# A hybrid encoder layer: normalised mixer operand, float32 SSM output operator, gates ahead of the attention, the per-layer projection moved to the FFN boundary

## The chip, the cores and the metric

The kernel runs on one core of one Trainium2 chip. The metric is device microseconds of one execution, the median of several runs. The engines are named PE (TensorE), DVE (VectorE), ACT (ScalarE), POOL (GpSimd) and SP (SyncE, which here only issues DMAs).

## The reference, cut to what is computed

One layer on 512 tokens of width 1024, all in float32:

```python
h = x
h = h + 0.5 * swiglu(rms_norm(h, ffn1_norm), ffn1_w_gate, ffn1_w_up, ffn1_w_down)   # width 2816
u = rms_norm(h, mix_norm)
q, k, v, x_ssm, g_attn, g_ssm = split(u @ w_in)          # 512, 128, 128, 512, 1024, 1024
q = rope(rms_norm(q)); k = rope(rms_norm(k))             # 8 query heads, 2 key/value heads of 64
y_attn = attention(q, k, v) @ w_attn_branch
y_s5 = s5_scan(x_ssm, forward) + s5_scan(x_ssm, reverse) + ssm_d * x_ssm   # 32 groups x 16, 64 states
z = gelu(y_s5)
z = z * sigmoid(z @ ssm_glu_w + ssm_glu_b)
y_ssm = z @ w_ssm_branch
h = h + (sigmoid(g_attn) * y_attn + sigmoid(g_ssm) * y_ssm) @ w_out
h = h + 0.5 * swiglu(rms_norm(h, ffn2_norm), ffn2_w_gate, ffn2_w_up, ffn2_w_down)
h = h + sigmoid(rms_norm(h, ple_norm) @ ple_w_gate) * (p @ ple_w_proj)     # p is 512 x 256
```

## The kernel before

**Layout and arithmetic.** The activation h is held transposed, features on partitions, as 8 tiles of 128x512. A large product works on float32r pairs: an operand is split into a high part, cast by ACT (L546), and a low part, subtracted by DVE (L547), and three matmuls (high by high, high by low, low by high; mm3, L560 to L563) go into one PSUM bank. wchunk (L549) loads a weight piece of at most 128x1024 over SP's queue (4 raw buffers, 4 split ones) and splits it so. The SSM's small products use bfloat16 triples with six matmuls (mm6, L43).

**Order.** Every engine has its own queue, in order. A scheduler fills the queues from the program's order as a priority; `tc.high_priority()` raises a piece, and a bank or a buffer with few copies holds its next user back. So the order that an engine sees differs from that of the code.

**Stages.** The input is loaded and transposed. FFN1 runs until 407.8 us; in its gaps a generator, ssm_params (L249 and after), computes the SSM's operators and writes them to DRAM: d_wv (input operator), d_wo (output operator), d_m (the part within a chunk) and d_tb (rotation and decay tables). Then the mixer:

- X, the SSM's input, is projected (proj_T, L785, 24 matmuls a tile, four tiles), goes to DRAM (xs_d) and comes back regrouped as U (L872), which is split into three bfloat16 parts (L875). rb, the row of 1/rms of all tokens, is made by the matmul pb from a diagonal matrix dg (L594 to L602) and multiplied in where a bank is copied out: X (L866), the gates (L816); K, V and Q take it per token as the scale of an ACT copy (L881, L883, L891).
- K and V, then Q, are projected with tokens on partitions (proj_tok, L801). Q and K get their head norm (msq, rqk, L894 to L897) and rope; both are transposed to qT, kh and kl. Q's head norm rq is not multiplied into Q but into the row maxima (L941) and the scale of the exponential (L943).
- Sixteen SSM blocks of two groups (ssm_block, L445): 24 bfloat16 matmuls pv, two rotations and two scans on DVE, a split of the state E into three bfloat16 parts (L481), then 12 matmuls with ml and 24 with wol into py; GELU writes a part of Z. ssm_prefetch (L428) loads a block's four operators over SP; wv has one buffer, the others two.
- The 16 gates (L812) are tanh of projections of 24 matmuls each. Eight (NG1) follow Q in the code, four (NG2) stand between the blocks, four fill the attention.
- The attention works head by head: scores (sc, L935 to L945), then values (L976): 16 transposes ppt, a split of each bank, eight matmuls po. Every head runs beside a filler, fill(i) (L1045): first the last four gates, then two halves of the GLU, whose operand zT comes from DRAM (z_load, L1007), then four halves of the SSM branch. The reciprocal row sums go to r_d (L949) and come back broadcast as R (L999), over SP; so do Z's stores (L966) and zT.
- The attention branch (96 matmuls) and w_out (192) end at 762.85 us.

FFN2 follows, and the tail: p is transposed (L1111), the gate product pge (192 matmuls) and the projection ple (48, L1143) are made per half of the width, combined (L1145 to L1148) and stored.

Of the kernel before, what the change touches and what calls it, by code (L numbers as in the profile page):

```python
# [45 lines left out]
def ssm_params(tc, nc, pk_, px, dp, k):  # L46
# [6 lines left out]
    d["wo"] = dp.tile([NB, P, 3 * GB * 2 * P], BF16, name="d_wo")  # L53
# [263 lines left out]
    bds = [pw.tile([P, 2, GB, 2, CH], F32, name=f"bd{i}") for i in range(2)]  # L317
# [110 lines left out]
def ssm_prefetch(nc, sp, k, j):  # L428
# [3 lines left out]
    wv = sp.tile([P, 3, GM, 2 * P], BF16, tag="wv", name=f"wv{j}")  # L432
# [768 lines left out]
```

## Time and profile before

| | |
|---|---|
| median of 3 runs | 1190.06 us (1187.46 to 1190.89) |
| the profiled execution | 1190.98 us, its span 1189.2 us |
| PE busy | 1145.6 us, 96% |
| DVE busy | 772.0 us, 65% |
| ACT busy | 501.6 us, 42% |
| POOL busy | 44.0 us, 4% |
| X's first and K's first matmul | 407.82, 431.43 us |
| first SSM product | 457.7 us |
| head 0's last score, attention's end | 583.49, 697.6 us |
| w_out's end | 762.85 us |

Times in the timeline count from the start of the span. A matmul's printed duration is longer than the distance to the next one, since matmuls overlap; where a dense stretch is priced, starts are subtracted. "Busy" of a group is the sum of its instructions, and the words behind the bar tell how long the engine had idled ahead of them and what ended that.

### The profile page before, as it was taken

How to read it: one execution, taken by the hardware profiler on the slowest of the kernel's cores; microseconds unless marked ns; L12 is line 12 of the kernel's file. 1: busy time of each engine (PE TensorE's matmuls, PEld its weight loads, DVE VectorE, ACT ScalarE, POOL GpSimd, SP SyncE). 2: the span in 40 equal slices, each digit the busy share in tenths (PEclk: the TensorE clock that was granted, in tenths of full speed). 3: DMA queues.
4: the chain of work that ended last, by engine and by line, in shares of the span. 5: the costliest groups of instructions: out<-in, count | busy, mean ns of one | idle time of the engine just before them, and what ended most of it. 6: DMA issues, size and time to landing. Idle time of an engine off the chain costs nothing.

```text
span 1189.2 us, 16474 instructions
## 1 busy us (share of the span) xinstructions
PE 1145.6 (96%) x6150; PEld 943.5 (79%) x6150; DVE 772.0 (65%) x1574; ACT 501.6 (42%) x915; POOL 44.0 (4%) x70
## 2 busy tenths in 40 slices
PE   8999989999999998988997999999999999999998
PEld 7788768888788887776785788888888888888886
DVE  4797589977688756999667857554443344444542
ACT  6475355544345435534465634333222223223331
POOL 4004300000000000000000000000000000000100
PEclk9999989999999999999998999999999999999999
DMA  9639956546967977887632135333323433223422
GB/s 199 142 93 275 283 181 199 173 137 138 280 216 259 280 195 145 243 257 228 162 95 51 45 85 172 89 100 96 90 63 97 140 91 105 79 72 98 154 59 53
DMA packets 258496, 175.97 MB, mean 148 GB/s; under 512 B 38928, under 2 KB 239824, under 8 KB 258416
## 3 DMA queue, kind: packets, MB, share of 16 engines
q1 hardware_dynamic: 254032, 162.66, 48.1%
q0 software_dynamic: 3920, 11.15, 3.7%
q10 hardware_dynamic: 464, 1.11, 0.4%
q8 instruction: 48, 0.79, 0.3%
q14 instruction: 32, 0.26, 0.1%
HBM read 148.89 MB, written 37.58 MB: 157 GB/s over the span
## 4 chain that ended last, share of the span: by engine, by line
PE 73%; DMA 10%; DVE 7%; SPq 3%; ACT 3%; issue 3%; ACTq 0%; DVEq 0%
PE pd L562 7%; PE pd L561 7%; PE pd L563 7%; PE pg L561 7%; PE pg L562 7%; PE pg L563 7%; PE pu L561 5%; PE pu L563 5%; PE pu L562 5%; DMA d_tb<-tst 3%; DMA wv<-d_wv 2%; DMA w<-in_ffn_w_up_dram 2%; PE pi L561 2%; PE pi L563 2%; PE pi L562 2%
## 5 line engine op out<-in xcount | busy, mean ns | idle before, releaser
L708 DVE TENSOR_TENSOR t<-pu,rb 128x512 f32<-128x512 f32 x44 | 30.3, 688 | 82.5 <-PE pu L563 82.3
L706 DVE TENSOR_TENSOR t<-pg,rb 128x512 f32<-128x512 f32 x44 | 30.3, 688 | 54.5 <-PE pg L563 52.5
L546 ACT CAST ah<-t 128x512 fp32r<-128x512 f32 x44 | 27.4, 622 | 42.3 <-DVE t L709 42.2
L726 DVE SCALAR_TENSOR_TENSOR h<-pd,h 128x512 f32<-128x512 f32 x32 | 22.0, 686 | 29.3 <-PE pd L563 29.3
L707 ACT ACTIVATE t<-t 128x512 f32<-128x512 f32 x44 | 27.8, 632 | 30.9 <-DVE t L706 30.3
L547 DVE TENSOR_TENSOR al<-t,ah 128x512 fp32r<-128x512 f32 x44 | 30.1, 685 | 7.1 <-ACT ah L546 7.0
L940 DVE TENSOR_REDUCE nb<-sc 128x1 f32<-128x512 f32 x32 | 21.6, 684 | 16.6 <-PE sc L939 16.5
L709 DVE TENSOR_TENSOR t<-t,t 128x512 f32<-128x512 f32 x44 | 30.3, 688 | 2.3
L943 ACT ACTIVATE p<-sc,nb,rq 128x512 f32<-128x512 f32 x32 | 24.8, 782 | 9.7 <-DVE nb L941 9.6
L547 DVE TENSOR_TENSOR pl<-ppt,ph 128x512 fp32r<-128x512 f32 x32 | 21.9, 684 | 6.6 <-ACT ph L546 6.6
L571 ACT ACTIVATE xh<-h,gains 128x512 fp32r<-128x512 f32 x24 | 17.4, 724 | 18.2 <-DVE h L726 17.8
L43 PE MATMUL pv<-U,wv 128*128 128x64 bf16 x384 | 14.0, 194 | 11.4 <-DMA wv<-d_wv 8.2
L1106 POOL DMA_DIRECT2D pin<-in_p_dram x8 | 4.2, 527 | 550.7 <-PE pd L562 545.5
L546 ACT CAST ph<-ppt 128x512 fp32r<-128x512 f32 x32 | 18.7, 589 | 12.8 <-PE ppt L983 12.6
L43 PEld LDWEIGHTS <-wv 128*128 128x128 bf16 x384 | 12.3, 98 | 14.3 <-DMA wv<-d_wv 10.0
L983 PE MATMUL ppt<-ident,p 128*128 128x128 f32 x128 | 20.6, 277 | 2.0 <-ACT p L943 2.0
L983 PEld LDWEIGHTS ppt<-ident,p 128*128 128x128 f32 x128 | 16.5, 142 | 6.7 <-ACT p L943 2.4
L33 ACT CAST E<-vv 128x256 bf16<-128x256 f32 x16 | 6.5, 403 | 32.1 <-DVE vv L479 31.9
L989 PE MATMUL po<-pl,vhl 128*128 128x512 f32 x32 | 13.5, 422 | 4.8 <-DVE pl L547 4.8
L43 PE MATMUL py<-E,wol 128*128 128x64 bf16 x384 | 17.7, 193 | 0.5 <-DVE E L36 0.4
L572 DVE SCALAR_TENSOR_TENSOR xl<-h,gains,xh 128x512 fp32r<-128x512 f32 x24 | 17.9, 746 | 0.4
L988 PE MATMUL po<-ph,vhl 128*128 128x512 f32 x32 | 14.2, 443 | 3.3 <-ACT ph L546 3.3
(1969 smaller groups left out, 3888.0 us busy)
## 6 DMA issues: line engine op xcount, KB each, us to landing
w<-in_ffn_w_gate_dram SPq DMA_DIRECT2D x44, 512.0 KB
w<-in_ffn_w_up_dram SPq DMA_DIRECT2D x44, 512.0 KB
w<-in_w_in_dram SPq DMA_DIRECT2D x26, 512.0 KB
w<-in_ffn_w_down_dram SPq DMA_DIRECT2D x32, 384.0 KB
w<-in_ffn_w_down_dram SPq DMA_DIRECT2D x32, 320.0 KB
d_wo<-wo SPq DMA_DIRECT2D x8, 768.0 KB
d_wv<-wv SPq DMA_DIRECT2D x8, 768.0 KB
wv<-d_wv SPq DMA_DIRECT2D x16, 384.0 KB
```

The lines of the kernel that those rows point to most:

```text
L43: nc.tensor.matmul(o, a[i], b[j], start=start and n == 0, stop=stop and n == 5)
L546: S.copy(hi, src)
L547: V.tensor_sub(lo, src, hi.bitcast(F32))
L561: T.matmul(o, ah, bh, start=start, stop=False)
L562: T.matmul(o, ah, bl, start=False, stop=False)
L563: T.matmul(o, al, bh, start=False, stop=stop)
L706: V.tensor_mul(t1, gu[0], rb)
L707: S.activation(t1, t1, AF.Silu)
L708: V.tensor_mul(t2, gu[1], rb)
L709: V.tensor_mul(t1, t1, t2)
L943: S.activation(p_, sc, AF.Exp, bias=nb[:, t:t + 1], scale=rq[:, t, hd:hd + 1], accum_out=sm[:, t:t + 1])
L983: T.transpose(pt[:, t * P:(t + 1) * P], pr[t][:, kt * P:(kt + 1) * P], ident)
```

## The change

- **Normalised operand.** FFN1's end no longer writes the split operand of h times the gain. It only collects squares; then rb is made, and behind it, in a new pool "pf", each tile xn = h x gain x rb is made and split. So X, K, V and Q are copied from their banks unscaled by ACT, and a gate is one tanh from the bank.
- **The projection of p** moves from the tail to this boundary: 8 transposes, 48 matmuls; eight results po of 128x512 (four buffers) are copied by ACT and stored to DRAM (pe_d) over POOL's queue. They are read back over the same queue ahead of FFN2, and the tail combines from there.
- **d_wo in float32.** One operator of 256 KB a block instead of three bfloat16 ones of 384 KB; E is not split; four float32 matmuls of 128x64 a block instead of 24 bfloat16 ones. The generator's store moves, wt gets two buffers and bd one.
- **wv** has two buffers.
- **NG2 is 8:** no gate is left among the heads, and block 0 is issued after Q's last matmul.
- **rq is multiplied into Q** (four DVE operations of 128x512); the 32 small multiplications of L941 and the scale of the exponential go.
- **POOL's queue** takes Z's stores, in quarters after blocks 3, 7, 11 and 15 (32 DMAs), zT's loads, r_d's stores and R's loads. z_load is cut in two, the loads one filler earlier than the splits; hb is loaded earlier.

The diff, cut to its core:

```diff
-    d["wo"] = dp.tile([NB, P, 3 * GB * 2 * P], BF16, name="d_wo")
+    d["wo"] = dp.tile([NB, P, GB * 2 * P], F32, name="d_wo")
...
-    wv = sp.tile([P, 3, GM, 2 * P], BF16, tag="wv", name=f"wv{j}")
+    wv = sp.tile([P, 3, GM, 2 * P], BF16, tag="wv", bufs=2, name=f"wv{j}")
...
-    wo = sp.tile([P, 3, GM, 2 * P], BF16, tag="wo", bufs=2, name=f"wol{j}")
+    wo = sp.tile([P, GM, 2 * P], F32, tag="wo", bufs=2, name=f"wol{j}")
...
-    E3 = [sp.tile([P, 2, N], BF16, tag=f"E{i}", bufs=2, name=f"E3{j}_{i}") for i in range(3)]
-    split3(nc, sp, E, E3, "vv", f"Er{j}", 3)
...
-            mm6(nc, o, [wo[:, i, g, ri * P:(ri + 1) * P] for i in range(3)],
-                [e[:, ri, g * NC_:(g + 1) * NC_] for e in E3], False, ri == 1)
+            nc.tensor.matmul(o, wo[:, g, ri * P:(ri + 1) * P], E[:, ri, g * NC_:(g + 1) * NC_],
+                             start=False, stop=ri == 1)
...
-NG1, NG2 = 8, 4
+NG1, NG2 = 8, 8
...
+        with tc.tile_pool(name="pf", bufs=1, reuse_waits="tile") as pp:
+            with tc.high_priority():
+                rb = rstd_bcast(st.rt())
...
+                    S.copy(po, pe)
+                    nc.gpsimd.dma_start(pe_d[t, :, nh * 512:(nh + 1) * 512], po)
+            xg = xg_tiles("x", KT)
+            with tc.high_priority():
+                for m in range(KT):
+                    xn = pp.tile([P, SEQ], F32, tag="xn", bufs=2, name=uid("xn"))
+                    V.scalar_tensor_tensor(xn, h[m], gains[:, 1, m:m + 1], rb, mul, mul)
+                    split(xg[m][0], xg[m][1], xn)
...
-            V.tensor_mul(dst, pg, rb)
-            S.activation(dst, dst, AF.Tanh, scale=0.5)
+            S.activation(dst, pg, AF.Tanh, scale=0.5)
...
+        for t in range(TT):
+            V.tensor_mul(qs[t], qs[t], rq[:, t].unsqueeze(2).broadcast_to([P, NH, HD]))
...
-            V.tensor_mul(nb[:, t:t + 1], nb[:, t:t + 1], rq[:, t, hd:hd + 1])
-            S.activation(p_, sc, AF.Exp, bias=nb[:, t:t + 1], scale=rq[:, t, hd:hd + 1], accum_out=sm[:, t:t + 1])
+            S.activation(p_, sc, AF.Exp, bias=nb[:, t:t + 1], accum_out=sm[:, t:t + 1])
...
-            nc.sync.dma_start(r_d[hd // 2].rearrange("h (t p) -> p h t", p=P), s2)
+            nc.gpsimd.dma_start(r_d[hd // 2].rearrange("h (t p) -> p h t", p=P), s2)
...
-        with tc.high_priority():
+        with tc.high_priority(), (tc.issue_after(last_q.ins) if j == 0 else ExitStack()):
...
+        if j % 4 == 3:
+            gs = slice((j - 3) * GM, (j + 1) * GM)
+            for l in range(L):
+                nc.gpsimd.dma_start(zv[l][:, gs], Z[l * CH:(l + 1) * CH, gs])
...
-                nc.sync.dma_start(R[i * HD:(i + 1) * HD], r_d[hd // 2][i].partition_broadcast(HD))
+                nc.gpsimd.dma_start(R[i * HD:(i + 1) * HD], r_d[hd // 2][i].partition_broadcast(HD))
...
-            nc.sync.dma_start(zT, zs_d[m * P:(m + 1) * P])
+            nc.gpsimd.dma_start(zTs[m], zs_d[m * P:(m + 1) * P])
...
+    pes = [lp.tile([P, D], F32, name=f"pes{t}") for t in range(TT)]
+    for t in range(TT):
+        nc.gpsimd.dma_start(pes[t], pe_d[t])
...
-                pe = bank("pv", uid("ple"))
-                for k in range(2):
-                    mm3(pe, pT[k][0][:, tk], pT[k][1][:, tk], ph[:, k], pl[:, k], k == 0, k == 1)
-                V.scalar_tensor_tensor(sg, sg, 1.0, pe, add, mul)
+                V.scalar_tensor_tensor(sg, sg, 1.0, pes[t][:, cs], add, mul)
```

What stands in the queues, first ACT's at the boundary between FFN1 and the mixer, before (w_... are weights' high parts, rb the row of 1/rms, ks and vs the copies of K and V):

```order
L546 CAST w_311h_4346<-w_311_4345 128x1024
L546 CAST w_312h_4400<-w_312_4399 128x1024
L546 CAST w_329h_4518<-w_329_4517 128x1024
L601 COPY rb_286_4114<-pb_285_4112 128x512
L546 CAST w_330h_4548<-w_330_4547 128x1024
L881 ACTIVATE ks0_4453<-pk0_4341,rs_282_4092 128x128
```

and after (po: the copies of the projection's banks ple; xh: high parts of the normalised operand):

```order
L794 COPY po_279_4130<-ple_278_4123 128x512
L794 COPY po_281_4140<-ple_280_4133 128x512
L794 COPY po_283_4150<-ple_282_4143 128x512
L794 COPY po_285_4160<-ple_284_4153 128x512
L544 CAST w_337h_4389<-w_337_4388 128x1024
L794 COPY po_288_4176<-ple_287_4169 128x512
L794 COPY po_290_4186<-ple_289_4179 128x512
L599 COPY rb_270_4085<-pb_269_4083 128x512
L794 COPY po_292_4196<-ple_291_4189 128x512
L544 CAST xh_295_4209<-xn_311_4225 128x512
```

rb stood behind weights' casts alone; now it stands behind six po copies, of which the fifth and sixth reuse the buffers of the first two.

SP's queue in the middle of the SSM blocks, before (tblN, wvN, mlN, wolN are block N's operators, w_... a gate's weights):

```order
L436 DMA tbl5_5599<-d_tb_282 128x5x128
L437 DMA tbl5_5599<-d_tb_282 128x128
L433 DMA wv5_5597<-d_wv_279 128x3x512
L441 DMA ml4_5509<-d_m_281 128x3x256
L556 DMA w_379_5384<-in_w_in_dram 128x8x128
L439 DMA wol4_5507<-d_wo_280 128x3x512
L436 DMA tbl6_5727<-d_tb_282 128x5x128
L437 DMA tbl6_5727<-d_tb_282 128x128
L433 DMA wv6_5725<-d_wv_279 128x3x512
```

and after, from block 2's wv on:

```order
L433 DMA wv2_5362<-d_wv_280 128x3x512
L433 DMA wv3_5429<-d_wv_280 128x3x512
L554 DMA w_393_5095<-in_w_in_dram 128x8x128
L436 DMA tbl2_5364<-d_tb_283 128x5x128
L437 DMA tbl2_5364<-d_tb_283 128x128
L433 DMA wv4_5528<-d_wv_280 128x3x512
L433 DMA wv5_5603<-d_wv_280 128x3x512
L441 DMA ml2_5369<-d_m_282 128x3x256
L439 DMA wol2_5367<-d_wo_281 128x512
```

Block N's wv stood behind block N's tables; now the wv of two blocks are asked for ahead of the tables of the first of them.

PE's queue where head 0's scores end and its transposes begin, before (sc: scores, ppt: transposes of the exponentials p, pi: a gate's bank):

```order
L938 MATMUL sc_393_6646<-kh_295_4139,qT_287_4131 128x512
L939 MATMUL sc_393_6646<-kl_297_4141,qT_287_4131 128x512
L983 MATMUL ppt_396_6752<-ident_69,p_388_6630 128x128
L561 MATMUL pi_400_6767<-xh_35_379,w_399h_6762 128x512
L562 MATMUL pi_400_6767<-xl_36_380,w_399h_6762 128x512
L563 MATMUL pi_400_6767<-xh_35_379,w_399l_6763 128x512
L561 MATMUL pi_400_6767<-xh_37_381,w_399h_6762 128x512
L562 MATMUL pi_400_6767<-xl_38_382,w_399h_6762 128x512
```

and after:

```order
L972 MATMUL sc_431_6505<-kh_327_4283,qT_319_4275 128x512
L973 MATMUL sc_431_6505<-kl_329_4285,qT_319_4275 128x512
L972 MATMUL sc_433_6511<-kh_327_4283,qT_319_4275 128x512
L973 MATMUL sc_433_6511<-kl_329_4285,qT_319_4275 128x512
L1018 MATMUL ppt_440_6596<-ident_69,p_428_6497 128x128
L972 MATMUL sc_444_6606<-kh_327_4283,qT_320_4276 128x512
L973 MATMUL sc_444_6606<-kl_329_4285,qT_320_4276 128x512
L1018 MATMUL ppt_446_6614<-ident_69,p_428_6497 128x128
L1018 MATMUL ppt_440_6596<-ident_69,p_430_6503 128x128
L1018 MATMUL ppt_446_6614<-ident_69,p_430_6503 128x128
```

The gate's matmuls that stood between head 0's transposes now stand ahead of its scores; behind them scores of head 1 alternate with the transposes.

## Rows read from the trace of the kernel before

**Rows 1.** The page's first part: busy time, share of the span, instructions.
```profile
PE 1145.6 (96%) x6150; PEld 943.5 (79%) x6150; DVE 772.0 (65%) x1574; ACT 501.6 (42%) x915; POOL 44.0 (4%) x70
```

**Rows 2.** Timeline, TensorE, 407 to 515: start us, us, engine line op operands.
```profile
407.59 0.39 PE L563 MATMUL pd<-ah,w_278l 128*128 128x512 f32 x1
...
415.75 0.95 PE L622 MATMUL pm<-ones,ss 128*128 128x1 f32 x8
...
416.56 0.49 PE L563 MATMUL pi<-xh,w_302l 128*128 128x512 f32 x1
...
428.94 1.02 PE L599 MATMUL pb<-dg,ones 128*128 128x512 f32 x2
...
442.97 0.40 PE L561 MATMUL pq<-w_329h,xh 128*128 128x512 f32 x1
...
513.79 0.86 PE L43 MATMUL pv<-U,wv 128*128 128x64 bf16 x24
...
514.49 0.34 PE L43 MATMUL py<-U,ml 128*128 128x64 bf16 x6
```

**Rows 3.** Timeline, VectorE and ScalarE, in the stretch of X.
```profile
423.08 0.16 DVE L584 TENSOR_TENSOR rs<-rs,rs 128x4 f32<-128x4 f32 x1
...
423.28 0.88 DVE L597 TENSOR_SCALAR dg<-ident,rs 128x128 f32<-128x128 f32 x4
...
430.00 0.59 ACT L601 COPY rb<-pb 128x512 f32<-128x512 f32 x1 [3.84 <-PE pb L599]
```

**Rows 4.** Timeline, TensorE, in the tail: first and last of 24 matmuls.
```profile
1178.27 0.39 PE L561 MATMUL ple<-w_1019h,pT 128*128 128x512 f32 x1
...
1183.48 0.39 PE L563 MATMUL ple<-w_1019h,pT 128*128 128x512 f32 x1
```

**Rows 5.** Stages: stretch, length, busy PE PEld DVE ACT POOL, granted clock, DMA share, GB/s.
```profile
431.43:583.72 152.29, 138.63 (x1473) 116.82 (x1472) 127.47 (x301) 68.58 (x195) 0.76 (x1) 0.98 0.77 206
583.72:697.60 113.88, 103.19 (x494) 82.35 (x494) 77.61 (x147) 68.56 (x133) 0.00 (x0) 0.96 0.32 71
484.00:514.00 30.00, 27.44 (x286) 22.48 (x285) 29.46 (x86) 11.88 (x36) 0.00 (x0) 1.00 0.85 255
514.00:544.00 30.00, 25.57 (x373) 21.85 (x369) 27.53 (x62) 13.32 (x28) 0.00 (x0) 1.00 0.90 262
623.00:643.00 20.00, 12.03 (x46) 8.59 (x45) 12.37 (x24) 10.10 (x21) 0.00 (x0) 0.74 0.38 56
```

**Rows 6.** Groups, 425 to 600: busy us, mean ns | idle before, releasers.
```profile
L477 DVE TENSOR_TENSOR te<-W,tbl 128x512 f32<-128x512 f32 x16 | 11.0, 685 | 0.1
...
L478 DVE TENSOR_TENSOR vv<-te 128x128 f32<-128x128 f32 x16 | 4.7, 291 | 0.2
...
L36 DVE TENSOR_TENSOR E<-Er,E 128x256 bf16<-128x256 f32 x16 | 6.8, 422 | 1.2 <-ACT E L35 0.9
...
L547 DVE TENSOR_TENSOR w_379l<-w,w_379h 128x1024 fp32r<-128x1024 f32 x1 | 1.2, 1225 | 0.5 <-ACT w_379h L546 0.5
...
L43 PE MATMUL py<-E,wol 128*128 128x64 bf16 x384 | 17.7, 193 | 0.5 <-DVE E L36 0.4
...
L43 PE MATMUL pv<-U,wv 128*128 128x64 bf16 x384 | 14.0, 194 | 11.4 <-DMA wv<-d_wv 8.2 <-DVE U L36 3.2
```

**Rows 7.** DMA issues of GpSimd's queue: count, KB each, median us to landing.
```profile
d_a<-d_at POOLq DMA_DIRECT2D x16, 256.0 KB, 10.8
...
d_bt<-sb POOLq DMA_DIRECT2D x2, 256.0 KB, 4.4
...
pin<-in_p_dram POOLq DMA_DIRECT2D x8, 64.0 KB, 2.4
```

**Rows 8.** Attention: a row of TensorE's timeline, two of the chain of waits.
```profile
585.88 0.33 PE L983 MATMUL ppt<-ident,p 128*128 128x128 f32 x1 [2.00 <-ACT p L943]
...
611.51 0.44 PE ppt L983 x4
...
622.27 11.60 DMA zT<-zs_d
```

More of the change, by code (lines that the diff above doesn't have):

```diff
@@ L316, in ssm_params @@
     kt = sm([P, 2, G, CH], "kt", pool=pk_)
-    bds = [pw.tile([P, 2, GB, 2, CH], F32, name=f"bd{i}") for i in range(2)]
+    bds = [pw.tile([P, 2, GB, 2, CH], F32, name=f"bd{i}") for i in range(1)]
     for bd in bds:
@@ L562, in mm3 @@
         T.matmul(o, ah, bl, start=False, stop=False)
-        T.matmul(o, al, bh, start=False, stop=stop)
+        return T.matmul(o, al, bh, start=False, stop=stop)
     def xg_tiles(tagp, n):
@@ L627 @@
     h_d = dp.tile([KT, P, SEQ], F32, name="h_d")
+    pe_d = dp.tile([TT, P, D], F32, name="pe_d")
     xg = xg_tiles("x", KT)
@@ L769 @@
             pass
-        xg = xg2
-        rt = st.rt()
-        rb = rstd_bcast(rt)
+        px_.close()
+        with tc.tile_pool(name="pf", bufs=1, reuse_waits="tile") as pp:
+            with tc.high_priority():
+                rb = rstd_bcast(st.rt())
+            pvw = w["p"][0, 0].rearrange("(c l) d -> l c d", l=L)
+            pin = [pp.tile([P, PLE], F32, name=f"pin{j}") for j in range(TT)]
+            for j in range(TT):
+                for i in range(2):
+                    nc.gpsimd.dma_start(pin[j][i * 64:(i + 1) * 64], pvw[2 * j + i])
+            pT = [tuple(pp.tile([P, SEQ], F32R, name=uid("pT")) for c in "hl") for k in range(2)]
+            for k in range(2):
+                pt = bank("pt", uid("pTp"))
+                for j in range(TT):
+                    T.transpose(pt[:, j * P:(j + 1) * P], pin[j][:, k * P:(k + 1) * P], ident)
+                split(pT[k][0], pT[k][1], pt)
+            for nh in range(2):
+                ph, pl = wchunk(w["ple_w_proj"][0][:, nh * 512:(nh + 1) * 512], 2, 512)
+                for t in range(TT):
+                    tk = slice(t * P, (t + 1) * P)
+                    pe = bank("mm", uid("ple"))
+                    for k in range(2):
+                        mm3(pe, pT[k][0][:, tk], pT[k][1][:, tk], ph[:, k], pl[:, k], k == 0, k == 1)
+                    po = pp.tile([P, 512], F32, tag="po", bufs=4, name=uid("po"))
+                    S.copy(po, pe)
[6 more added lines that the diff above has]
+                    split(xg[m][0], xg[m][1], xn)
     win = w["w_in"][0]
@@ L826 @@
     vhl = mp.tile([P, TT, 2, 2, HD], F32R, name="vhl")
-    rq = mp.tile([P, TT, NH], F32, name="rq")
     sx = ExitStack()
@@ L963 @@
             run(scores(0))
-    zv = zs_d.rearrange("(g c) (l n) -> l c g n", c=CH, l=L)
-    for l in range(L):
-        nc.sync.dma_start(zv[l], Z[l * CH:(l + 1) * CH])
     sx.close()
@@ L1048, in fill @@
             return gate(NG1 + NG2 + i)
-        if i < ng + 2:
-            if i == ng:
-                z_load()
-            return half(w["ssm_glu_w"][0], i - ng, [z[1:] for z in zs[1:]], glu_done)
-        if i < ng + 6:
-            return half(w["w_ssm_branch"][0], i - ng - 2, yhl, ssm_done)
+        i -= ng + 2
+        if i < 0:
+            if i == -2:
+                zl.append(z_load())
+            next(zl[0], None)
+            return iter(())
+        if i < 2:
+            return half(w["ssm_glu_w"][0], i, [z[1:] for z in zs[1:]], glu_done)
+        if i < 6:
+            return half(w["w_ssm_branch"][0], i - 2, yhl, ssm_done)
         return iter(())
@@ L1074 @@
         run(values(hd), fill(hd), *([scores(hd + 1)] if hd < NH - 1 else []))
-    for i in range(NH, 2 * KT - NG1 - NG2 + 6):
+    for i in range(NH, 2 * KT - NG1 - NG2 + 8):
         run(fill(i))
@@ L1090 @@
     mx.close()
+    lp = ctx.enter_context(tc.tile_pool(name="lp", bufs=1, reuse_waits="tile"))
+    pes = [lp.tile([P, D], F32, name=f"pes{t}") for t in range(TT)]
+    for t in range(TT):
+        nc.gpsimd.dma_start(pes[t], pe_d[t])
     with tc.tile_pool(name="f2", bufs=1, reuse_waits="tile") as fp:
```

62 lines of the change are left out of this document (28 added, 34 removed).

## The prediction

> **What bounds the kernel now.** I read the page's busy line first, then stretches of the timeline, the busy times by stage, the groups of the SSM stage and the issues of GpSimd's queue. TensorE is busy 96% of the span, 43.6 us short of all of it [rows 1], so time moves where its work shrinks or its idle time does. The two FFNs and w_out keep their work. That leaves three places: the boundary behind FFN1, the mixer from the first K matmul to the end of the attention, and the tail. In the mixer the stretch to head 0's last score takes 152.29 us with 138.63 of TensorE, the attention behind it 113.88 with 103.19 [rows 5]. In the first VectorE is the other limit: in the 30 us from 484 it is busy 29.46, with the DMA engines at 0.85 and 255 GB/s; in the next 30, 27.53 at 0.90 and 262 GB/s [rows 5]. The idle time in front of the SSM's first product, 11.4 us, ends on loads of wv for 8.2 and on U's split for 3.2 [rows 6]: the single wv buffer.
>
> One float32r 128x512 matmul is worth (1183.48-1178.27)/23 = 0.2265 us [rows 4]. One gate is 24 of them, 5.44.
>
> The sum goes by the profiled run, 1190.98 us (1189.2 span, 1.8 around it), which stands 0.9 above the median of the runs, 1190.06.
>
> **The tail: -11.0.** The 48 projection matmuls leave it: 48 x 0.2265 = 10.9 on TensorE, of which the last 24 stand at the very end [rows 4]. The eight transposes go too (8 x 0.11 = 0.9, by 0.44 for four [rows 8]), but some ran in gaps; I count 0.1 of them. Behind the last pge matmul tanh, two VectorE operations and the output stores remain, as they remain now behind the last ple. The projection is read back from DRAM under the whole of FFN2.
>
> **The boundary: +15.0.** Before, X's 96 matmuls follow FFN1's last one (pd at 407.59 [rows 2]) without a gap and K starts at 431.43, because the norm was applied only at the copies: rb came at 430.00 [rows 3], under cover. Now nothing of X can start before rb, and the projection is the cover: 10.9 + 0.9 = 11.8 of TensorE. The norm's chain behind the last down-projection: sum and square about 2 us, pm 0.81 (415.75 to the next matmul at 416.56 [rows 2]), 14 small operations at 0.20 (423.08 to 423.28), dg 0.88, pb 1.0, rb 0.59, then xn and its cast some 1.3 [rows 2, 3]: about 9.6, under the 11.8. I add 1.2 for the cast of pT, behind which the projection waits, and 2.0 for ScalarE's order. There rb stands behind the copies of the fifth and sixth projection tile, po_288 and po_290, and these need the buffers of the first two back (four in all), that is, stores on GpSimd's queue landed. Issued about 4.5 and 6 us after the down-projection, they land 2.4 us later by pin (64 KB, quiet), 4.4 by d_bt (256 KB), 10.8 by d_a (256 KB, queue and DMA engines loaded) [rows 7]. I take 4.4: the size of po, and in this stretch the queue holds little else. Ends: +13 with nothing waiting, +21.4 by d_a.
>
> **From K to the end of attention: -8.9.**
> K and Q are unchanged: 96 matmuls of 256 columns in 442.97-431.43 = 11.5 us [rows 2], 96 of 512 in 21.8, together 33.3. Block 0 is now issued after Q's last matmul, so X's way through DRAM to U lies under these 33.3, and U's 3.2 us of waiting [rows 6] goes.
> Removed in every block: the split of E, two casts on ScalarE and two VectorE subtractions (0.422 for the last [rows 6]), 16 x 0.84 = 13.5 us of VectorE; twelve gate multiplications at 0.685 in this stage, 8.2. Added: four multiplications of rq into qs, 2.7. What VectorE keeps: per block four operations of 128x512 or a scan at 0.685 and four of 128x128 at 0.29, so 3.9, times 16 = 62.4; Q's rope, 4 x (2 x 0.685 + 2 x 0.42) = 8.8; eight qT of that size, 5.5; nine lo halves of weights at 1.225 = 11.0 [rows 6]. With 2.7 that is 90.4.
> The loads: 1216 KB a block (wo is 256 KB, was 384) and 512 KB a gate, 2944 KB for a pair of blocks and its gate. At 262 GB/s that is 11.5 us, against VectorE's 2 x 3.9 + 1.2 = 9.0. The first three pairs carry the rope and qT and are VectorE's; over the last five the loads are 12.5 behind. A second wv buffer draws some forward into the early pairs; I take a third of 12.5, about 4, as what stays: the stage is 94. Ends: 87 (VectorE's operations start a little before the one ahead ends) and 103.
> The E products: 384 bf16 matmuls of (514.49-513.79)/24 = 0.0293 [rows 2], 11.2, become 64 float32 ones. Nothing before runs that shape; pm, four float32 matmuls of one column (each recorded as two) in 0.81, says 0.20 each, 12.8 in all. By columns alone pb (one float32 matmul of 512 columns, 1.02 [rows 2]) gives an eighth of its time, 0.13, so 8.2; both added give 0.33, 21. I take pm's, since 64 columns are nearer to 1 than to 512. TensorE has 8 x 5.44 for gates, 16 x 36 x 0.0293 = 16.9 for bf16 and these 12.8 to do in the 94, 73 us, so the 1.6 more, or 10, stay covered.
> By the Trainium skill ("FP8 and Floating Point Precision", "TensorE Precision Notes") true float32 takes four passes through the array; by that alone the 64 products would be 6.8 us (an estimate from 64 columns a pass), and the sum would be the same, since they are covered.
> The gates: eight in the stage (before, twelve came before the end of it), eight behind the last block, of which three quarters of one still fill block 15's chain: 7.25 x 5.44 = 39.4. So 33.3 + 94 + 39.4 = 166.7, against 152.29.
> The attention has no gate left in it. Its content: 128 products of heads and 144 of GLU and branch halves, 272 x 0.2265 = 61.6, and 128 transposes at 0.11 (0.44 for four [rows 8]) = 14.0: 75.6. Before, with four gates, 97.4 of 113.88, so 16.5 idle or slow. Of that 8.0 is idle time in the 20 us from 623, where TensorE is busy 12.03 and waits, through ScalarE's order, for zT, 11.6 us on SP's queue [rows 5, 8]; its granted clock there, after idling, is 0.74, part of the stretch at 1.2 GHz instead of 2.4. That goes: Z is stored in quarters from GpSimd's queue, and zT is asked for a step before it is used. What is late next: the first heads' softmax. Before, a gate covered it after 2.00 us of idling [rows 8]; now head 0's transposes come directly behind its scores, and each tile waits for maximum, exponential and casts: I take 7 for heads 0 and 1, 2 for a clock that falls there, 1.5 in the middle, 4.5 for the last head's chain to oT, which no gate covers: 15. Ends 9 and 22. So 75.6 + 15 = 90.6.
> Both stages: 166.7 + 90.6 = 257.3, against 152.29 + 113.88 = 266.2.
>
> **The rest at nothing.** ScalarE's plain copies replace scaled ones of the same size. In FFN1 the two wt buffers and the single bd change the filler's pace, which TensorE's own work hides; a stall there is VectorE's. The 32 Z stores and eight r stores and loads leave SP, on which the weights queue.
>
> **Sum.** -11.0 + 15.0 - 8.9 = -4.9: 1190.98 - 4.9 = 1186.1, on the scale of the median **1185.2**, say 1185.
>
> **The rivals.**
> A, slower: the boundary. rb waits on stores that land as d_a's did, 10.8 instead of 4.4: +6.4; TensorE, idle that long in two pieces, comes back at 1.2 GHz, and the 20 us at 0.74 [rows 5] lost up to 0.26 x 20 = 5.2, so I price that 4. 1185.2 + 10.4 = 1195.6. It turns slower from a landing of 12.8 alone, or from about 9 with the clock. For it: FFN1's weights and X's share these DMA engines, and the copies, the norm and X's splits are all in one order. Against it: pin landed in 2.4, and so few transfers are on that queue at a time.
> By the Trainium skill ("SBUF — State Buffer", "SBUF: two separate sides") certain VectorE operations lock GpSimd out of a shared port, so that it cannot write the descriptors of its own queue's transfers; by it this move of stores and R loads to GpSimd is the wrong way, and A gains. The 10.8 of FFN1 doesn't tell such a stall from full DMA engines.
> B, no change: the loads set the SSM pace whatever wv's buffers: tbl, wo and m keep two each, on one queue in order, so a wv asked for early stands behind a table that has no buffer. Then four of the five late pairs take 11.5: 90 + 10 = 100, +6, 1191. For it: DMA at 0.90 in the late stretch [rows 5].
> C, more: VectorE alone sets the stage, 87 (-7), and the attention idles 9 (-6): 1172. For it: VectorE's 29.46 of 30; the loads need 24 MB in all, 92 us at 262, which speaks against.
>
> **How the numbers follow.** Forecast 0.40 (1178 to 1188), B 0.22, A 0.20, C 0.18. A measurement tells about 0.3% from no change, 3.6 us: faster below 1186.5, slower above 1193.6. Faster: 0.34 of the forecast and C's 0.18, 0.52; same: 0.06 and 0.19 of B, 0.25; slower: A and 0.03 of B, 0.23. The range leaves out a tenth on either side: half of C below 1168, half of A above 1198.
>
> **What would show it.** Right: first X product 13 to 16 us after the last pd; U no releaser; block period late about 5.4; seven gates in a row, 38 to 40 us of unbroken TensorE; zT landed before the GLU; no ple in the tail, sg straight behind pge; E products near 0.20. Wrong: rb or po waiting on a store of pe_d for over 5 us; wv still named before pv; a granted clock well under 1 behind the boundary or at the first ppt; TensorE idle over 20 us in the attention.

## The result and the profile after

The changed kernel takes 1195.79 us (median of 6 runs, 1193.75 to 1201.7) where the kernel before takes 1190.05: ratio 1.0055 (95% interval 1.0036 to 1.0074), slower by 0.55%, some 6.5 us (the medians stand 5.7 apart). I had forecast 1185, in a range of 1178 to 1188.

The profiled run is 1195.75 us, its span 1193.9, against 1190.98 and 1189.2. The page's first line answers to [rows 1]:

```profile
PE 1154.7 (97%) x5894; PEld 951.3 (80%) x5894; DVE 755.2 (63%) x1501; ACT 491.7 (41%) x895; POOL 77.4 (6%) x130
```

TensorE is busy 9.1 us longer, VectorE 16.8 us shorter. Cut at the same matmuls as before, the difference of the spans, 4.7 us, lies as follows:

| stretch (TensorE) | before | after | difference | forecast |
|---|---|---|---|---|
| start to the first matmul behind FFN1 | 407.82 | 406.52 | -1.3 | 0 |
| from there to X's first matmul | 0 | 15.38 | +15.4 | +15.0 |
| X, to K's first matmul | 23.61 | 21.94 | -1.7 | 0 |
| K to head 0's last score | 152.29 | 177.15 | +24.9 | +14.4 |
| attention, its branch and w_out | 179.13 | 157.85 | -21.3 | -23.3 |
| FFN2 and tail | 426.35 | 415.06 | -11.3 | -11.0 |

One row failed, the fourth. Its 10.5 us over the forecast are 8.5 in the block stage and 2.1 of head 0's scores, which the forecast had in the attention, less 0.1 in the gates. Stages of the changed kernel, with the columns of [rows 5]: K and Q, the SSM blocks (first pv to last py), the gates behind them, the attention, and three stretches of 5 us inside the blocks:

```profile
443.84:477.14 33.30, 33.30 (x193) 29.35 (x192) 17.98 (x38) 19.21 (x62) 0.00 (x0) 1.00 0.92 164
477.14:579.60 102.46, 92.55 (x940) 79.77 (x940) 87.25 (x215) 30.78 (x93) 12.57 (x24) 0.92 0.78 230
579.60:618.87 39.27, 39.27 (x175) 32.47 (x174) 8.57 (x7) 11.07 (x16) 5.77 (x11) 1.00 0.33 101
620.99:713.60 92.61, 87.28 (x427) 68.91 (x426) 68.11 (x105) 59.04 (x125) 7.88 (x12) 0.98 0.24 57
500.00:505.00 5.00, 2.72 (x58) 2.20 (x58) 4.82 (x17) 1.54 (x2) 0.00 (x0) 0.94 1.08 311
505.00:510.00 5.00, 5.00 (x35) 4.90 (x33) 4.11 (x14) 0.56 (x2) 0.00 (x0) 0.50 1.09 314
570.00:575.00 5.00, 4.25 (x13) 2.90 (x12) 4.64 (x8) 1.75 (x3) 0.00 (x0) 0.50 0.00 0
```

K and Q take the 33.3 us that I gave them, and the gates behind the blocks run for 39.27 without a gap (forecast 39.4). The block stage takes 102.46 instead of 94. VectorE is busy 87.25 of it, near my 90.4, which leaves 15.2 us that it does not fill. TensorE is busy 92.55, which is only 9.9 us of idling, but its granted clock is 0.92 (1.00 is 2.4 GHz, 0.50 is 1.2): a part of the stage ran at 1.2 GHz, at most 0.08 x 102.46 = 8.2 us of work lost. The timeline of TensorE shows how it goes, start, duration, operands and the idle time before:

```profile
502.33 1.12 PE L43 MATMUL pv<-U,wv 128*128 128x64 bf16 x33 [1.00 <-DVE tt L463]
504.74 0.50 PE L43 MATMUL py<-U,ml 128*128 128x64 bf16 x6 [1.29 <-DMA ml<-d_m]
505.05 2.00 PE L485 MATMUL py<-vv,wol 128*128 128x64 f32 x8
506.84 0.85 PE L43 MATMUL py<-U,ml 128*128 128x64 bf16 x12
...
509.20 0.77 PE L559 MATMUL pi<-xh,w_385h 128*128 128x512 f32 x1
```

A wait of 1.00 us for VectorE (pv's bank) and one of 1.29 for ml, and from 505 to 510 the granted clock is 0.50: eight records of float32 products take 506.84 - 505.05 = 1.79 us, twice what they take at 2.4 GHz (below). The same again behind the idling for K's transposes, which wait for banks that VectorE's qT work holds:

```profile
565.36 0.35 PE L43 MATMUL py<-U,ml 128*128 128x64 bf16 x6 [0.20 <-DMA ml<-d_m]
569.33 1.11 PE L951 MATMUL kt<-ident,kd 128*128 128x128 f32 x4 [3.62 <-DVE qT L942]
...
572.31 0.76 PE L559 MATMUL pi<-xh,w_409h 128*128 128x512 f32 x1 [0.42 <-DVE qT L942]
```

At full clock the float32 product shows its price. Four records, two matmuls, go from 524.51 to 524.98 and from 525.16 to 525.60:

```profile
524.51 0.64 PE L485 MATMUL py<-vv,wol 128*128 128x64 f32 x4
524.98 0.34 PE L43 MATMUL py<-U,ml 128*128 128x64 bf16 x6
525.16 0.64 PE L485 MATMUL py<-vv,wol 128*128 128x64 f32 x4
525.60 0.48 PE L560 MATMUL pi<-xl,w_387h 128*128 128x512 f32 x1
```

That is 0.22 to 0.24 for one of the 64, 14.4 us in all, where I took 0.20 and 12.8.

The boundary, TensorE first, then ScalarE:

```profile
406.52 1.04 PE L784 MATMUL pTp<-ident,pin 128*128 128x128 f32 x8
408.66 0.50 PE L559 MATMUL ple<-w_277h,pT 128*128 128x512 f32 x1 [1.10 <-ACT pT L544]
...
418.25 1.02 PE L597 MATMUL pb<-dg,ones 128*128 128x512 f32 x2
...
421.90 0.50 PE L559 MATMUL pi<-xh,w_331h 128*128 128x512 f32 x1
```

```profile
418.03 0.59 ACT L794 COPY po<-ple 128x512 f32<-128x512 f32 x1 [0.32 <-DMA pe_d<-po]
418.90 0.59 ACT L794 COPY po<-ple 128x512 f32<-128x512 f32 x1 [0.29 <-DMA pe_d<-po]
419.38 0.59 ACT L599 COPY rb<-pb 128x512 f32<-128x512 f32 x1
```

The projection fills the time from 408.66 to X's first matmul at 421.90. The two po copies do wait for stores of pe_d, but for 0.32 and 0.29 us, not 2.0 together, since these stores land in 3.1:

```profile
pe_d<-po POOLq DMA_DIRECT2D x8, 256.0 KB, 3.1
```

In the tail the last pge matmul is the last one, and no ple follows:

```profile
1187.52 0.39 PE L561 MATMUL pge<-w_1047h,xl 128*128 128x512 f32 x1
```

The attention's own idle places are those that I named, the bare start behind head 0's scores and the last head's chain to oT:

```profile
620.76 0.40 PE L973 MATMUL sc<-kl,qT 128*128 128x512 f32 x1
624.25 0.47 PE L1018 MATMUL ppt<-ident,p 128*128 128x128 f32 x1 [3.09 <-ACT p L976]
```

```profile
714.46 0.49 PE L1024 MATMUL po<-pl,vhl 128*128 128x512 f32 x1 [0.23 <-DVE pl L545]
717.72 0.79 PE L559 MATMUL pg<-oT,w_671h 128*128 128x512 f32 x1 [2.76 <-ACT oT L544]
```

### The profile page after: what moved, and what is told of

It reads as the page before. It is cut to its first block, busy times and chain, and to the rows that moved or that the text cites. A ratio compares the mean times of both kernels' runs of the same rounds, so it can differ in the third digit from the quotient of the medians.

```text
span 1193.9 us, 15946 instructions
## 1 busy us (share of the span) xinstructions
PE 1154.7 (97%) x5894; PEld 951.3 (80%) x5894; DVE 755.2 (63%) x1501; ACT 491.7 (41%) x895; POOL 77.4 (6%) x130
## 4 chain that ended last, share of the span: by engine, by line
PE 74%; DMA 9%; issue 5%; DVE 5%; ACT 4%; SPq 3%; POOL 0%; ACTq 0%; DVEq 0%; POOLq 0%
PE pg L559 7%; PE pg L560 7%; PE pg L561 7%; PE pd L559 6%; PE pd L560 6%; PE pd L561 6%; PE pu L559 5%; PE pu L560 5%; PE pu L561 5%; DMA d_tb<-tst 2%; DMA w<-in_ffn_w_up_dram 2%; DMA tbl<-d_tb 1%; PE pi L559 1%; SPq L403 1%; PE pi L560 1%
## 5 line engine op out<-in xcount | busy, mean ns | idle before, releaser
L997 POOL DMA_DIRECT2D zs_d<-Z x32 | 16.8, 531 | 142.6 <-ACT Z L993 141.3
L993 ACT ACTIVATE Z<-py 128x128 f32<-128x128 f32 x16 | 4.4, 278 | 50.7 <-PE py L485 50.3
L544 ACT CAST ph<-ppt 128x512 fp32r<-128x512 f32 x32 | 18.5, 590 | 12.2 <-PE ppt L1018 11.8
L485 PE MATMUL py<-vv,wol 128*128 128x64 f32 x128 | 22.0, 305 | 0.7 <-DMA wol<-d_wo 0.7
L976 ACT ACTIVATE p<-sc,nb 128x512 f32<-128x512 f32 x32 | 22.0, 698 | 1.3 <-DVE nb L974 1.0
L610 ACT ACTIVATE sqv<-h 128x512 f32<-128x512 f32 x24 | 14.9, 622 | 13.1 <-DVE h L725 13.1
L485 PEld LDWEIGHTS py<-vv,wol 128*128 128x128 f32 x128 | 19.2, 215 | 1.3 <-DVE w_411l L545 0.8
L1125 DVE SCALAR_TENSOR_TENSOR h<-po,h 128x512 f32<-128x512 f32 x8 | 5.5, 690 | 16.7 <-PE po L561 16.7
L972 PE MATMUL sc<-kh,qT 128*128 128x512 f32 x32 | 14.6, 456 | 0.8 <-ACT p L976 0.6
```

Source lines behind the costliest of these rows:

```text
L485: nc.tensor.matmul(o, wo[:, g, ri * P:(ri + 1) * P], E[:, ri, g * NC_:(g + 1) * NC_], start=False, stop=ri == 1)
L544: S.copy(hi, src)
```

## The experiments

Every ratio is to the kernel before, run on the same chip beside it; the changed kernel's own is 1.0055 (1.0036 to 1.0074). 0.1% is 1.2 us. Edits are to the changed kernel. The scheduler places the work anew for each edit, so an edit's effect includes that of the order that it brings.

| run | edit | ratio (95% interval) |
|---|---|---|
| e1 | operators of 14 blocks not loaded | 1.0000 (0.9986 to 1.0013) |
| e2 | four gates among the heads | 1.0138 (1.0123 to 1.0154) |
| e3 | bfloat16 output operator, one wv | 0.9968 (0.9951 to 0.9985) |
| e4 | projection in the tail | 1.0149 (1.0128 to 1.0169) |
| e5 | one wv | 1.0000 (0.998 to 1.002) |
| e6 | block j behind gate j-1 | 1.0018 (1.0001 to 1.0036) |
| e7 | block j behind gate j-2 | 1.0025 (1.0002 to 1.0047) |
| e8 | GpSimd's transfers on SP | 1.0089 (1.0062 to 1.0115) |
| e9 | block 0 not held behind Q | 1.0083 (1.0054 to 1.0112) |
| e10 | K's transposes first | 1.0046 (1.0024 to 1.0068) |
| e11 | e3, block 0 not held | 1.0024 (0.9995 to 1.0052) |
| e12 | e3, K's transposes first | 0.9969 (0.9943 to 0.9995) |
| e13 | e5, E's products twice | 1.0085 (1.0052 to 1.0118) |
| e14 | e5, E split again, unused | 1.0013 (0.9995 to 1.0032) |
| e15 | e3, block j behind gate j-2 | 0.9946 (0.9929 to 0.9963) |
| e16 | e5, three ml buffers | 0.9961 (0.9948 to 0.9974) |
| e17 | e16, block j behind gate j-2 | 0.9997 (0.9974 to 1.002) |

**The output operator and wv (e3, e5).** In e3:

```diff
-    wv = sp.tile([P, 3, GM, 2 * P], BF16, tag="wv", bufs=2, name=f"wv{j}")
+    wv = sp.tile([P, 3, GM, 2 * P], BF16, tag="wv", name=f"wv{j}")
...
-    wo = sp.tile([P, GM, 2 * P], F32, tag="wo", bufs=2, name=f"wol{j}")
+    wo = sp.tile([P, 3, GM, 2 * P], BF16, tag="wo", bufs=2, name=f"wol{j}")
...
+    E3 = [sp.tile([P, 2, N], BF16, tag=f"E{i}", bufs=2, name=f"E3{j}_{i}") for i in range(3)]
+    split3(nc, sp, E, E3, "vv", f"Er{j}", 3)
...
-            nc.tensor.matmul(o, wo[:, g, ri * P:(ri + 1) * P], E[:, ri, g * NC_:(g + 1) * NC_],
-                             start=False, stop=ri == 1)
+            mm6(nc, o, [wo[:, i, g, ri * P:(ri + 1) * P] for i in range(3)],
+                [e[:, ri, g * NC_:(g + 1) * NC_] for e in E3], False, ri == 1)
```

> The output operator as before: three bfloat16 parts (384 KB a block), E split (13.5 us of VectorE), 384 small products; wv with one buffer, since two don't fit beside it. If loads and VectorE set the block stage: 2.1 MB more at 0.26 MB a us and 13.5 us of VectorE lengthen it by 8 to 13, 1204 to 1209. If float32 E products (0.225 us each, 14.4 for 64 against 11.2) and what waits behind them set it: 1190 to 1194.

Measured 0.9968, 1184.2 us: these two parts of the change cost 0.87%, 10 us, and all the others together gain. My expectation by loads and VectorE, 8 to 13 us slower, is out by 20 us and of the wrong sign; the other branch, 1190 to 1194, is missed too. Then e5, the first two lines of that diff alone:

> The changed kernel with one wv buffer in place of two, the float32 operator kept. In the order of TensorE's queue this holds the blocks back: block 15's first product then stands behind 12.8 of the 16 gates, where the changed kernel has it behind 7.5. Theory of crowding (blocks too fast for their loads, eight gates left over behind them): like e3, TensorE keeps work between the blocks and its clock, 1181 to 1187. Theory of the float32 products (their time, and what stands behind them): 1192 to 1197. Theory of wv (a second buffer takes waits away): slower than the changed kernel, 1198 to 1204.

1.0000, in none of my three ranges: taken out in this order, the second wv buffer costs 0.55% of the 0.87 (give or take 0.3), the float32 operator 0.32 (about 4 us, give or take 3). Where the blocks stand shows in the span of pv, in the changed kernel, in e3 and in e5 (the two times are the first and the last start):

```profile
L43 PE MATMUL pv<-U,wv x384: 189/193/242, 477.1 to 557.3; 128*128 128x64 bf16 x192
```

```profile
L43 PE MATMUL pv<-U,wv x384: 193/193/203, 476.0 to 589.5; 128*128 128x64 bf16 x192
```

```profile
L43 PE MATMUL pv<-U,wv x384: 193/193/242, 477.2 to 594.9; 128*128 128x64 bf16 x192
```

With two wv buffers the sixteen blocks run in 80 us and leave some seven gates behind them, in one piece in which VectorE is busy 8.57 of 39.27 us; with one they take 113 us in e3 and 118 in e5, and more of the gates stand between them. All of Q to w_out, in the changed kernel and in e3, and three stretches of e3 around its longest waits:

```profile
455.35:778.84 323.49, 305.11 (x1899) 249.77 (x1898) 222.09 (x413) 141.05 (x309) 29.04 (x52) 0.96 0.51 138
```

```profile
454.23:765.66 311.43, 293.10 (x2155) 238.11 (x2154) 233.84 (x444) 151.44 (x341) 29.07 (x52) 0.99 0.53 149
534.00:539.00 5.00, 2.34 (x60) 2.07 (x59) 3.07 (x8) 2.10 (x4) 0.00 (x0) 1.00 0.72 213
540.00:545.00 5.00, 2.44 (x65) 2.19 (x63) 4.83 (x10) 3.52 (x9) 0.45 (x1) 1.00 0.92 271
545.00:550.00 5.00, 3.98 (x46) 3.34 (x47) 4.82 (x10) 1.64 (x3) 3.73 (x8) 1.00 0.92 265
```

The idle time is the same, 323.49 - 305.11 = 18.4 and 311.43 - 293.10 = 18.3. The 12 us between them are busy time: 3.2 for the products (14.4 against 11.2), and the rest goes with the granted clock, 0.96 against 0.99 (up to 0.04 x 323 = 12.9 and 0.01 x 311 = 3.1 us of work lost). e3 idled over 5 us between 534 and 545 and was granted 1.00 throughout; the changed kernel, after 2.3 us, fell to 0.50. The spread alone does not keep the clock: e5's blocks are spread as wide as e3's, and it idles 16.2 us from Q to w_out at a granted clock of 0.96 (its row stands below, with e13 and e14).

**The spacing (e6, e7).** The blocks are tied to the gates, j to gate j-1 in e6 and to gate j-2 in e7, and gate j follows block j in the code from the eighth on:

```diff
-        with tc.high_priority(), (tc.issue_after(last_q.ins) if j == 0 else ExitStack()):
+        with tc.high_priority(), tc.issue_after((gl[j - 1] if j >= 1 else last_q).ins):
...
-        if j % 2 == 0 and j // 2 < NG2:
-            run(gate(NG1 + j // 2))
+        if j >= NG1:
+            run(gate(j))
+            gl.append(last_g[0])
```

> The changed kernel, two wv buffers, but block j is issued behind gate j-1's last matmul, so that one gate stands between any two blocks and none behind the last. Theory of crowding: TensorE's 20.8 us idle or at the lower clock between Q and head 0's scores (141.7 us for 120.9 of work) fall to about 8: 1181 to 1185. If the loads hold the pace whatever the order: 24 MB in 130 us is no bound, so this theory too says faster, but with waits on ml and tbl still named for over 5 us: 1187 to 1191. If each block's chain is longer than a gate and simply idles TensorE: 1195 or more.

> As e6, but block j behind gate j-2's last matmul, one block of slack. Theory of crowding: like e6, or up to 2 us better, since a late load meets a started block: 1180 to 1185. If the spacing as such is not what matters: 1194 to 1197.

1.0018 and 1.0025: faster than the changed kernel by 4.4 and 3.6 us (give or take 3 and 3.5) with the second wv in place, so where the blocks stand is a part of it, but not the 10 to 15 that the theory of crowding promised. In e6 a wait of 5 us for K's transposes and a clock of 0.59 behind it remain.

**The loads (e1, e16).** e1 keeps the first two sets of operators:

```diff
-            pre = ssm_prefetch(nc, sp, kd, j + 1)
+            pre = pres[(j + 1) % 2] if j else pres.append(ssm_prefetch(nc, sp, kd, 1)) or pres[1]
```

> The changed kernel, but only the operators of SSM blocks 0 and 1 are loaded and all sixteen blocks use these two sets (14 sets of 1216 KB, 17 MB, are left out; the SSM's result is then another one). If the loads set the pace of the block stage (102.5 us from the first pv at 477.1 to the last py at 579.2, where I had 94): no wait on ml, wol or tbl is left, the 7 us of TensorE's waits on them and VectorE's 5.2 on tbl go, with some 5 us at the lower clock behind them: 10 to 14 us less, 1182 to 1186. If VectorE's 87 us or the chain of one block sets it: 1194 to 1197, and the waits get other names.

1.0000, 6.5 us less: no wait for an operator is left, and then VectorE does set the pace of the blocks. Its row from 490 to 560, then the blocks' first and last products:

```profile
490.00:560.00 70.00, 64.35 (x752) 55.81 (x751) 67.99 (x182) 16.31 (x44) 12.61 (x24) 1.00 0.27 62
```

```profile
L43 PE MATMUL pv<-U,wv x384: 189/193/203, 479.8 to 549.0; 128*128 128x64 bf16 x192
...
L485 PE MATMUL py<-vv,wol x128: 222/275/323, 491.6 to 563.8; 128*128 128x64 f32 x128
```

VectorE is busy 67.99 us of 70. The block stage is 84 us long (479.8 to 563.8), 18 shorter than in the changed kernel, and yet the kernel gains only 6.5: gates that no longer run between the blocks run behind them. So the length of the stage is not what is paid. The loads' share is below the 10 to 14 that I expected. e16 gives e5 a third buffer for ml (`tag="m", bufs=3`):

> e5 with a third buffer for ml, so that its load can be asked for a block earlier. e5's TensorE waits for ml 1.2 and 2.3 us, for wv and wol 2.5 in all. If these waits are the price of SP's order: 0.996 to 0.998. If another load is late in their place: 0.999 to 1.002.

0.9961, 4.6 us better than e5 and 0.94% better than the changed kernel, with the float32 operator kept. That is level with e3's 0.9968, so with a third ml buffer no cost of the float32 operator shows. The bfloat16 operator with three ml buffers was not tried.

**What TensorE's and VectorE's time is worth (e13, e14).** e13 makes each product of E twice in e5, e14 makes the unused split:

```diff
+            for r in range(2):
+                nc.tensor.matmul(o, wo[:, g, ri * P:(ri + 1) * P], E[:, ri, g * NC_:(g + 1) * NC_],
+                                 start=False, stop=ri == 1 and r == 1)
```

> e5 (one wv, float32 operator; ratio 1.000 to the kernel before) with each of the 64 float32 products of E made twice into the same bank, 14.4 us more on TensorE at 0.225 each and nothing else (the SSM's result is then another one). If TensorE's work in the block stage counts in full: ratio 1.010 to 1.013, 12 to 15 us. If VectorE or the loads pace the stage, as I predicted, and the products are covered: 1.000 to 1.003.

> e5 with the split of E made in every block as the kernel before makes it and its result not used: 13.5 us more of VectorE (32 subtractions of 128x256) and 32 casts of ScalarE, TensorE's work unchanged. If VectorE paces the stage, as I predicted: ratio 1.008 to 1.012. If TensorE sets it and VectorE has room: 0.998 to 1.002; below 0.998 if a slower block is even spaced better.

e13: +0.85% over e5, 10 us (give or take 4.6) for 14.4 of TensorE's, a little under the range for full payment. The products are not covered. e14: +0.13%, inside the intervals, for 13.5 us of VectorE. The rows from Q to w_out, e5, then e13, then e14:

```profile
455.42:775.34 319.92, 303.77 (x1898) 247.99 (x1897) 223.26 (x412) 140.94 (x309) 28.98 (x52) 0.96 0.52 141
```

```profile
454.24:781.34 327.10, 313.02 (x2026) 258.22 (x2025) 223.77 (x412) 140.96 (x309) 29.09 (x52) 0.98 0.50 137
```

```profile
455.23:775.12 319.89, 303.93 (x1898) 248.04 (x1897) 234.17 (x444) 151.80 (x341) 29.10 (x52) 0.96 0.51 140
```

In e14 VectorE is busy 10.9 us longer than in e5, ScalarE 10.9, TensorE as long as before, and so is the stretch. In e13 the stretch is 7.2 us longer and the granted clock 0.98 against 0.96, so a part of the products' time may have come back through the clock. Both edits stand on e5, whose blocks are spread; on the changed kernel, where VectorE has less room (it idles 0.5 us for pv there, 17.0 in e5), neither was made.

**The other parts (e4, e2, e8, e9, e11).** e4 puts transposes and projection back into the tail:

> The projection of p back in the tail, the normalised operand kept. Then nothing covers the norm's chain at the boundary: by my working 9.6 us of idle time in place of 15.4 us, and the tail is 11.0 longer: +5 to +6, 1201 to 1202, and up to 4 more if TensorE comes back at the lower clock, 1205. If the norm's chain is shorter than the projection by much (5 or 6 us): 1196 to 1198.

1.0149, 0.94% slower than the changed kernel, just past the end of the range that I gave with the clock (1205; measured 1205.88). The norm's chain stands bare:

```profile
404.84 0.39 PE L561 MATMUL pd<-ah,w_262l 128*128 128x512 f32 x1
408.05 1.05 PE L620 MATMUL pm<-ones,ss 128*128 128x1 f32 x8 [2.81 <-DVE ss L615]
412.85 2.08 PE L597 MATMUL pb<-dg,ones 128*128 128x512 f32 x2 [3.75 <-DVE dg L595]
417.03 0.80 PE L559 MATMUL pi<-xh,w_307h 128*128 128x512 f32 x1 [2.11 <-ACT xh L544]
```

12.2 us from the last pd to X, of which 8.67 are idle, and a lower clock behind it (pb takes 2.08). So the projection as a cover is worth some 11 us (give or take 3), twice the 5 to 6 that my working gave without the clock. e2 is `NG1, NG2 = 8, 4`:

> NG2 back to 4: four of the gates stand among the heads again, all else as changed. If the bare heads cost what the trace shows (17 us idle or at the lower clock in the attention, where the kernel before had 16.5 with 8 of them a wait for zT that is gone now): the attention idles about 8, total 1186 to 1189. If the gates behind the blocks only changed place and the idle time follows them: 1194 to 1197.

1.0138, slower by 0.83%, above both ranges that I gave. The wait for zT is back, now on GpSimd's queue, where it lands in 13.2 us, and in the changed kernel in 4.4:

```profile
640.33 0.60 PE L1018 MATMUL ppt<-ident,p 128*128 128x128 f32 x4
650.26 0.80 PE L1023 MATMUL po<-ph,vhl 128*128 128x512 f32 x1 [9.34 <-ACT ph L544]
```

```profile
zT<-zs_d POOLq DMA_DIRECT2D x4, 256.0 KB, 13.2
```

```profile
zT<-zs_d POOLq DMA_DIRECT2D x4, 256.0 KB, 4.4
...
r_d<-s POOLq DMA_DIRECT2D x4, 4.0 KB, 11.4
```

So e2 does not show what a gate among the heads covers, since zT's wait hides it. Why the same loads landed so much later there was not tried; in e2 they are issued among the stores and loads of the reciprocals, at 635 to 640. e8 takes all of GpSimd's new transfers but pe_d's back to SP (`nc.gpsimd` to `nc.sync` in four lines):

> The changed kernel with Z's stores, zT's loads, the reciprocals' stores and loads back on SP's queue. If GpSimd's queue starves beside VectorE (the rule of the Trainium skill on the shared port, rival A's ground): faster, 1190 to 1194. If SP's order was the trouble (weights queued behind r_d's stores and 32 issues at 0.53 us): slower, 1198 to 1204. If neither is on the path: 1195 to 1197.

1.0089, slower by 0.34%, at the edge of the intervals: GpSimd's queue is no loss and perhaps a gain, though r_d's store alone takes 11.4 us on it (row above). On SP, R's loads held that queue for these stores four times, 31.9 us in all. e9 drops the rule on block 0, e11 does so in e3:

```diff
-        with tc.high_priority(), (tc.issue_after(last_q.ins) if j == 0 else ExitStack()):
+        with tc.high_priority():
```

> The changed kernel without the rule that block 0 is issued after Q's last matmul; blocks start as soon as U is split. In the kernel before, the first pv started 14 us ahead of Q's end, in the changed one 0.2 behind it. If the blocks' late start is what took the gain (a chain of sixteen blocks compressed, its gates left behind it): the blocks end some 10 us earlier against Q, idle time falls, 1188 to 1192. If U's wait (3.2 us in the kernel before) comes back into Q's queue and the crowding of loads stays: 1196 to 1200.

> e3 (bfloat16 output operator, one wv) without the rule on block 0. e3 has a ratio of 0.9968 to the kernel before. If the early start of the blocks is worth something also where they are spread: 1178 to 1182 (0.990 to 0.994). If it is spread enough and U's wait returns: 1184 to 1189.

1.0083 and 1.0024: 0.28% slower than the changed kernel, which is inside the intervals, and 0.56% slower than e3, which is clear of them. I had thought that the late start took the gain; beside e3's parts it is one of those that bring it.

**No effect (e10, e12).** The block of kd2 and kt moves ahead of the loop of qt.

> The changed kernel with K's transposes (kt) ahead of Q's (qt) in the code. In the changed kernel kt waits 3.8 us, then 0.6 and 0.7, for banks that VectorE's qT subtractions hold, with a granted clock of 0.50 in the 5 us from 570. If the wait is K's alone: 4 to 8 us less, 1188 to 1192. If it only moves to the last qt, which then needs the banks: 1194 to 1197.

> e3 with K's transposes ahead of Q's. e3 lost 2.0 us there and kept its clock. If that is all: 1182 to 1184. If the order matters more through the blocks that stand behind: 1178 to 1181, or 1186 and more if the wait falls on qt.

1.0046 and 0.9969 against 1.0055 and 0.9968: within the intervals. The wait changes its place: in e10 the longest in this stretch is one of 4.3 us in front of a py product, for VectorE's vv.

**The fastest (e15, e17).** e15 is e3 with e7's spacing:

> e3 (ratio 0.997) with block j issued behind gate j-2's last matmul, as e7. If even spacing is worth what e7 showed of it against the changed kernel (3 us): 0.993 to 0.995. If e3's order is spaced already: 0.996 to 0.999.

0.9946, 1185.61 us where the kernel before takes 1191.02 on that chip: faster than both kernels, while the 0.22% against e3 is inside the intervals. e17 puts the spacing on e16:

> e16 (float32 operator, one wv, three ml; ratio 0.9961) with block j issued behind gate j-2's last matmul, as in e15. If the spacing is a remedy of its own: 0.992 to 0.994. If e16 owes its gain to the place of the blocks as much as to the loads, the two don't add: 0.995 to 0.998.

0.9997, above both ranges. The remedies do not add, which suggests that e16's gain is tied to where its blocks stand.

## Why the prediction was wrong, point by point

- **Tail and boundary: the totals are right, the boundary's in part by luck.** -11.3 for -11.0, +15.4 for +15.0. In the boundary two errors cancel: the pm and pb matmuls, 1.8, were left out (they leave X's stretch, hence its -1.7), and of the 2.0 for ScalarE's order only 0.6 came. The casts took as long as I said (1.10 of 1.2).
- **The block stage: wrong, 94 against 102.46.** This is the step that failed. I took the stage's length from VectorE (90.4, measured busy 87.25) and put the loads on top, added a fixed number of gates behind it, and took TensorE's work as covered by a stage that is longer than it. e1 shows on the changed kernel itself that this length is not what is paid: without the loads the stage is 18 us shorter, the kernel 6.5. e13 shows on e5 that TensorE's time in this stage is paid, at 10 us for 14.4, since whatever a gate doesn't do between the blocks it does behind them. e14, on e5 too, finds 13.5 us of VectorE worth 0.13%. So the float32 operator, whose VectorE saving I had in the sum, was a loss of its TensorE time: 3.2 us by the rows, 0.32% by e3 and e5, though beside three ml buffers (e16) no loss shows.
- **The second wv buffer: wrong sign.** I counted it as the end of [rows 6]'s waits. The waits on wv did end. But the blocks ran ahead of their other loads and of the gates: the waits took the names of ml (3.3 us of TensorE's), wol (0.7) and tbl (5.2 of VectorE's), and TensorE's clock fell behind some of them (e1: 6.5 us for all loads). e5 gives 0.55%, e6 and e7 0.37 and 0.30 by spacing alone. In which of these ways the buffer costs its time is argued, not shown.
- **The stage's list: short by 4.7 us.** qt and kt (24 transposes, 2.6) and head 0's scores (2.1, which I had in the attention) were not in it.
- **The attention: nearly right.** Its idle time was to be 15; TensorE was busy 87.28 of 92.61 at a clock of 0.98, for 73.8 of work without head 0's scores: 18.8 lost. zT's wait went as forecast, though e2 shows that GpSimd's queue alone does not see to that.
- **The rivals.** A, rb behind stores on GpSimd's queue, fell: 3.1 us landing, 0.6 of waiting. That its price, 1195.6, is what was measured is chance. The rule of the Trainium skill ("SBUF — State Buffer", "SBUF: two separate sides"), by which certain VectorE operations lock GpSimd out of a shared port, speaks of a stall that does not show here: pe_d's stores landed in 3.1 us, and e8, with Z's, zT's and the reciprocals' transfers on SP, is not faster. Whether such operations ran beside them no run tells. B had the right stage and nearly the right length for it (100), but not its whole cause: without any loads only 6.5 us come back. C fell.
- **The forecast's 1185** is about what e3 takes, 1184.2, which is the change without the two parts that I had mis-signed. That agreement is of the sums, and not evidence for my 94.

**Open.** What decides whether the granted clock falls behind a short idle piece. The clock from Q to w_out, in the profiled runs, is 0.94 to 0.97 in the changed kernel, e2, e4 to e11, e14 and e17, 0.98 or 0.99 in e1, e3, e12, e13, e15 and e16. Float32 and bfloat16 products are in both lists, and so are blocks that are crowded and blocks that are spread. It moves more time (up to 10 us) than the products do, and I could not tie it to an edit: of the 12 us between the changed kernel and e3 some 9 go with it. That the crowding causes it was the theory behind e5 to e7; it is not shown, and e5's 0.96 speaks against it as the whole cause.

## What to carry to other kernels

On an engine that is busy 97% of the span, an edit is priced by what it does to that engine's own work and to the pieces in which it idles; savings elsewhere count only where that engine waits for them, and work that seems covered in one stage is paid in the next one if filler is moved there. A buffer that takes a wait away can let its chain run ahead of the work that was to fill its gaps, so look where the filler goes before counting the wait as won. Work that must be done anyway is the best cover for a chain that can't be shortened: moving the projection to the boundary was worth 0.94%.

## What I had not expected of the hardware

- A float32 matmul of 128x64 costs about 0.225 us at full clock, nearly eight times the 0.0293 of a bfloat16 one, so six bfloat16 products (0.176) are cheaper than one in float32.
- The granted clock fell to 0.50 for 5 us behind idle pieces of 1.00 and 1.29 us, and stayed at 1.00 in e3, where TensorE was busy 2.34 and 2.44 of two stretches of 5 us. In the changed kernel itself an idle piece of 1.80 us left it at 1.00 (TensorE busy 3.19 of the 5 us from 530).
- The same four zT loads on the same queue landed in 4.4 us and in 13.2 (e2).
